# A trunk layer on one core: pools of their own for the first ffn_out's block sets, transposes at three norms at other steps, and groups of the mixing output that begin with the weight blocks still held

## The chip, the cores and the metric

The kernel runs on one core of one Trainium2 chip. The metric is the device time of one execution in microseconds (us). Three runs of the kernel before took 2295.66, 2296.3 and 2301.58 us; the median is 2296.3.

## The reference

One layer of an encoder trunk on 1024 tokens of width 1024, in float32: a half-step SwiGLU feed-forward part, a token mixing (retention in both directions, two-dimensional neighbourhood attention, gates), and a second feed-forward part, each between two RMS norms.

```python
def _rms_norm(x, gain):
    xf = x.astype(jnp.float32)
    y = xf * lax.rsqrt(jnp.mean(xf * xf, axis=-1, keepdims=True) + RMS_EPS)
    return (y * gain.astype(jnp.float32)).astype(x.dtype)

def _swiglu(x, w_in, w_out):
    g, u = jnp.split(x @ w_in, 2, axis=-1)
    return (jax.nn.silu(g) * u) @ w_out
...
    y_ret = (jax.nn.silu(rg) * y) @ w_ret_out
...
    merged = jax.nn.sigmoid(g_ret) * y_ret + jax.nn.sigmoid(g_na) * y_na
    return merged @ w_out
...
        h = _swiglu(_rms_norm(x, ffn1_pre_norm[l]), ffn1_w_in[l], ffn1_w_out[l])
        x = x + 0.5 * _rms_norm(h, ffn1_post_norm[l])
        m = _token_mixing(_rms_norm(x, mix_pre_norm[l]), w_mix_in[l], ret_decay_fwd[l], ret_decay_bwd[l],
                          na_rel_bias[l], w_ret_out[l], w_na_out[l], w_mix_out[l], pos)
        x = x + _rms_norm(m, mix_post_norm[l])
        h = _swiglu(_rms_norm(x, ffn2_pre_norm[l]), ffn2_w_in[l], ffn2_w_out[l])
        x = x + 0.5 * _rms_norm(h, ffn2_post_norm[l])
```

The hidden width of the feed-forward parts is 2816.

## The kernel before

**Precision.** Each float32 operand is split (`split`, L50) into a high part in fp32r, cast by ScalarE (L60), and a low part, the difference, by VectorE (L61). A product is three matmuls (`mm3`, L85, its lines L87 to L89): high by high, low by high, high by low. Names ending in h and l are such halves: wh and wl of a weight, gh and gl of a block of the hidden layer, a11h and a11l of an operand.

**Tokens.** The 1024 tokens are eight tiles of 128 rows, called tokens 0 to 7 here. Each stage begins with a norm and then *flips* a token: eight TensorE transposes (L126), four to a half, put the normalized rows into columns. `put` (L257) takes each half from its bank. For tokens 0 to 3 it is two splits. For tokens 4 to 7, ScalarE copies the first half (L272), and further sums (L276, L277, L282, L284, and L287, L288 on GpSimd) make the seven operands of a Strassen-Winograd scheme: a11, a12, a22, s1 to s4. Two banks, pt, serve the flips, six banks, ps, the products.

**ffn_in** (L404) computes the gate and up halves of the hidden layer in 22 steps, each with seven products of 12 matmuls. It stores blocks of the hidden layer (a11) and their sums to device memory, and beside that makes the four weight sums for ffn_out: `OutSums` (L509) loads four tiles tw, subtracts, and stores the result t. SyncE issues the loads (weights as wraw, blocks as graw), GpSimd the stores. Before the main loop, `lead` (L330) does the first two products of six of the steps, in between the norms of tokens 4 to 7; `norm_T` (L100) writes a normed token into tmp (L117).

**ffn_out** (L536) runs seven products over 11 blocks each. `Blocks` (L447) loads a block (graw) and splits it into gh and gl; which pool a set comes from goes round a list of four, and each pool reuses the memory of what was there before. In ffn_in 1's place lie, among others, the tiles tw; a set that lies over one must wait until the store that reads it has landed. While the last products run, the finished tokens go through stages (`Epilogue.steps`, L486): stage 0 sums the squares, 1 adds the residue (L494), 2 is the next norm (L505), 3 the flip. They lie in the list `later`, and one is taken per step. Tokens 4 to 7 finish last; their flips are done inside the mixing's first products by the loop at L1144, with 8 fillings of products in between. Before, all norms of 5, 6 and 7 stand at ffn_out's end.

**The mixing output** (`out_proj`, L136) goes through groups of tokens (0, 1, 2), (3, 4, 5), (6, 7). For each group it goes through the eight blocks k of the contraction; it loads and splits a weight block and the tokens' m (`stream`), and has the banks of the group's tokens summed. The last three k (`tail`) are kept, so that tokens end one after the other; each finished token goes through its epilogue (L219 to L230 on ScalarE, VectorE and, for tokens 6 and 7, GpSimd), its norm (L113, L117), and, `lag` products later, its flip.

The order on each engine is decided by a scheduler, from the order in which the code is written; `issue_after` holds an instruction behind a given one. Engines work through their queues in order.

## Time and profile before

| | |
|---|---|
| runs | 2295.66, 2296.3, 2301.58 us |
| the profiled execution | 2297.41 us |
| its span | 2295.6 us |
| mean granted clock | 0.991 |
| TensorE busy | 2216.4 us, 97% |
| VectorE, ScalarE, GpSimd busy | 1680.1, 1003.4, 591.6 us |

The span is what the profiler recorded from the first instruction to the last; 1.8 us of the execution lie around it. In the profile PE is TensorE, PEld its weight loads, DVE VectorE, ACT ScalarE, POOL GpSimd and SP SyncE; L with a number is a line of the kernel. A row of a window gives, for each engine, busy us and the count of its instructions, then the granted clock of TensorE (1.00 is full), the share of the DMA engines and GB/s. A row of waits gives who waits for whose result: us in total, times, the longest. A row of a timeline gives start, duration, the instruction, and in brackets the idle time before it and what ended that.

### The profile page before, as it was taken

To read this page: it belongs to the slowest core of one execution; us is meant where nothing else is said; L and a number is where in the kernel's file an instruction comes from. 1 tells how busy PE (TensorE), PEld (TensorE's weight loads), DVE (VectorE), ACT (ScalarE), POOL (GpSimd) and SP (SyncE) were. 2 spreads that over 40 slices of the span, in tenths; PEclk is the share of its full clock that TensorE was granted. 3 is DMA by queue.
4 is the path that set the end of the run, shared out by engine and by line. 5 is a ranking of instruction groups with operands and counts; after the bars stand their busy time and mean duration, and the time that the engine had idled before them with its cause. 6 is when DMAs were issued, how large, how long until landed. Compare 5 with 4: busy or idle time off the path is not lost.

```text
span 2295.6 us, 30372 instructions
## 1 busy us (share of the span) xinstructions
PE 2216.4 (97%) x10288; PEld 1838.0 (80%) x10288; DVE 1680.1 (73%) x2945; ACT 1003.4 (44%) x2102; POOL 591.6 (26%) x689
## 2 busy tenths in 40 slices
PE   6999999989998999999999999999799999999998
PEld 5788888768777887787888888887578888888886
DVE  7897777745778768969975688546899777776576
ACT  6333222334454322248885675315543222234453
POOL 5342424210124134411101222101533333331012
PEclk9999999999999999999999999999899999999999
DMA  5464545467664542257755476766545545447765
GB/s 183 148 215 142 174 144 176 153 217 235 196 208 137 179 166 103 92 182 244 223 176 172 150 228 233 277 230 206 180 157 177 181 145 183 134 167 232 235 199 184
DMA packets 163675, 422.63 MB, mean 184 GB/s; under 512 B 19712, under 2 KB 47488, under 8 KB 163456
## 3 DMA queue, kind: packets, MB, share of 16 engines
q1 hardware_dynamic: 130080, 310.04, 42.5%
q0 software_dynamic: 33440, 110.65, 12.5%
q8 instruction: 81, 1.33, 0.2%
q14 instruction: 74, 0.61, 0.1%
HBM read 301.60 MB, written 123.21 MB: 185 GB/s over the span
## 4 chain that ended last, share of the span: by engine, by line
PE 81%; DVE 11%; issue 3%; POOL 3%; ACT 1%; DMA 1%; POOLq 0%; DVEq 0%; SPq 0%; ACTq 0%
PE ps L89 25%; PE ps L87 25%; PE ps L88 25%; DVE wl L61 2%; PE pt L88 1%; PE pt L87 1%; PE pt L89 1%; PE ps L726 1%; POOL rstd L97 1%; PE pt L745 1%; POOL cmb L287 1%; POOL cmb L288 1%; DVE t L378 1%; DVE xs L494 1%; DVE tmp L117 1%
## 5 line engine op out<-in xcount | busy, mean ns | idle before, releaser
L61 DVE TENSOR_TENSOR wl<-wraw,wh 128x512 fp32r<-128x512 f32 x662 | 470.6, 730 | 77.8 <-ACT wh L60 76.9
L60 ACT CAST wh<-wraw 128x512 fp32r<-128x512 f32 x670 | 390.4, 618 | 218.5 <-PE ps L88 78.5
L87 PE MATMUL ps<-wh,gh 128*128 128x512 f32 x612 | 239.8, 393 | 13.2 <-ACT gh L60 12.0
L61 DVE TENSOR_TENSOR gl<-graw,gh 128x512 fp32r<-128x512 f32 (+2 forms) x178 | 128.4, 724 | 161.2 <-ACT gh L60 161.2
L88 PE MATMUL ps<-wl,gh 128*128 128x512 f32 x612 | 240.1, 393 | 2.0 <-DVE wl L61 2.0
L89 PE MATMUL ps<-wh,gl 128*128 128x512 f32 x612 | 239.4, 394 | 0.7 <-DVE gl L61 0.5
L60 ACT CAST gh<-graw 128x512 fp32r<-128x512 f32 (+2 forms) x178 | 106.6, 602 | 216.2 <-PE ps L88 86.8
L414 ACT ACTIVATE c<-c 128x512 f32<-128x512 f32 x88 | 55.7, 633 | 289.3 <-DVE c L384 206.4
L87 PEld LDWEIGHTS ps<-wh,gh 128*128 128x128 f32 x612 | 115.7, 189 | 39.1 <-ACT gh L60 13.1
L89 PEld LDWEIGHTS ps<-wh,gl 128*128 128x128 f32 x612 | 115.9, 190 | 28.0 <-DVE gl L61 3.9
L88 PEld LDWEIGHTS ps<-wl,gh 128*128 128x128 f32 x612 | 115.9, 190 | 25.9 <-DVE wl L61 2.7
L60 ACT CAST wh<-t 128x512 fp32r<-128x512 f32 x58 | 36.1, 622 | 201.8 <-DVE t L378 192.2
L484 POOL TENSOR_TENSOR q<-q,gain 128x512 f32<-128x512 f32 x22 | 33.6, 1544 | 348.7 <-ACT ps L483 334.4
L89 PE MATMUL ps<-a12h,wl 128*128 128x512 f32 x280 | 110.7, 395 | 3.7 <-DVE wl L61 3.7
L87 PE MATMUL ps<-a11h,wh 128*128 128x512 f32 x280 | 111.6, 399 | 1.4 <-ACT wh L60 0.7
L87 PE MATMUL ps<-a12h,wh 128*128 128x512 f32 x280 | 111.2, 397 | 0.0
L89 PE MATMUL ps<-a11h,wl 128*128 128x512 f32 x280 | 110.4, 394 | 0.7 <-DVE wl L61 0.7
L88 PE MATMUL ps<-a11l,wh 128*128 128x512 f32 x280 | 110.4, 394 | 0.0
L88 PE MATMUL ps<-a12l,wh 128*128 128x512 f32 x280 | 109.9, 392 | 0.0
L87 PE MATMUL ps<-a22h,wh 128*128 128x512 f32 x280 | 109.8, 392 | 0.0
L89 PE MATMUL ps<-a22h,wl 128*128 128x512 f32 x280 | 109.1, 390 | 0.0
L88 PE MATMUL ps<-a22l,wh 128*128 128x512 f32 x280 | 109.1, 389 | 0.0
(354 smaller groups left out, 5973.9 us busy)
## 6 DMA issues: line engine op xcount, KB each, us to landing
wraw<-in_dram SPq DMA_DIRECT2D x243, 512.0 KB, 4.4
tw<-in_dram SPq DMA_DIRECT2D x88, 256.0 KB, 3.3
t<-tw POOLq DMA_DIRECT2D x88, 256.0 KB, 4.1
wraw<-t SPq DMA_DIRECT2D x40, 512.0 KB, 3.8
g0s<-cmb POOLq DMA_DIRECT2D x44, 256.0 KB, 4.0
graw<-g0s SPq DMA_DIRECT2D x44, 256.0 KB, 2.9
g1s<-cmb POOLq DMA_DIRECT2D x44, 256.0 KB, 4.2
graw<-g1s SPq DMA_DIRECT2D x44, 256.0 KB, 2.8
```

Source lines behind the costliest of these rows:

```text
L60: nc.scalar.copy(h, src)
L61: (eng or nc.vector).tensor_tensor(l, src, hf, ALU.subtract)
L87: mm(ps, a[0], b[0], start=start, stop=False)
L88: mm(ps, a[0], b[1], start=False, stop=False)
L89: mm(ps, a[1], b[0], start=False, stop=stop)
L97: self.nc.gpsimd.tensor_tensor(r[:, :n], ms, self.mhalf[:, :n], ALU.pow)
L117: nc.vector.scalar_tensor_tensor(xn[:, bs], x[:, bs], r[:, 0:1], gain[:, bs], op0=ALU.mult, op1=ALU.mult)
L287: nc.gpsimd.tensor_tensor(s3, h2, s3, ALU.subtract)
L288: nc.gpsimd.tensor_tensor(s3, s3, l2, ALU.add)
L378: tt(t2, b22, t1, ALU.subtract)
L414: nc.scalar.activation(gate[j], gate[j], AF.Silu)
L484: (eng or c.nc.gpsimd).tensor_tensor(h if out is None else out, h, self.post[:, b * 512:(b + 1) * 512], ALU.mult)
```

## The change

Five things are changed.

1. **Block sets of the first ffn_out.** g0, g1 and g2 are the pools gl10, gl11 and gl12. The list of sets goes from (g0, g0, g0, g1) to (g0, g0, g1, g1), that of the raw blocks from (g2, g2, g1, g1) to (g2, g2, g0, g0), so that g1 holds sets alone. junk lies in front of them, two of the xs behind; tw is split into two pools of four tiles, for even and odd k.
2. **The start.** Tokens 0 to 3 are flipped at once, the flips of 4 to 7 are handed to `lead`, which does one after each of its pairs of products. tmp has four buffers instead of three; lead's results get a pool of their own.
3. **Stages in ffn_out.** A table, STAGES, mixes the stages of the four tokens instead of having token after token.
4. **Norms of tokens 6 and 7.** They are called in the flip loop, after the flips of tokens 4 and 5.
5. **The mixing output.** Each group but the first begins with the three weight blocks that the one before held, so 18 blocks are loaded instead of 24; the last group has a tail too; the flips are held behind the last matmul issued.

```diff
 RET_FILL = (14, 2, 2, 4, 2, 3, 0, 1, 2)
+STAGES = ((0, 0), (0, 1), (0, 2), (1, 0), (0, 3), (1, 1), (1, 2), (2, 0), (1, 3),
+          (2, 1), (2, 2), (3, 0), (3, 1), (2, 3), (3, 2), (3, 3))
 FLIP_FILL = (8, 8, 8, 8, 2)
 KEY_OFF = (0, 8, 24, 32)
...
         mm(ps, a[0], b[1], start=False, stop=False)
-        mm(ps, a[1], b[0], start=False, stop=stop)
+        return mm(ps, a[1], b[0], start=False, stop=stop)
         return self.psum.tile([P, 512], F32, tag=tag, name=tag, bufs=bufs)
...
-    def norm_T(self, x, gain, t, pool, put, ss=None):
+    def norm_T(self, x, gain, t, pool, put, ss=None, tmps=3):
...
         nc = self.nc
-        xn = pool.tile([P, D], F32, tag="tmp", name="tmp", bufs=3)
+        xn = pool.tile([P, D], F32, tag="tmp", name="tmp", bufs=tmps)
         if ss is None:
             for b in range(2):
...
-        left = []
-
-        def one(t, k, a, w):
+        left, last, mm = [], [], []
+
+        def one(t, k, a, w, start, stop):
             for e in [e for e in left if e[0] <= 0]:
                 left.remove(e)
-                f = e[1]()
+                with self.tc.issue_after(mm[0].ins):
+                    f = e[1]()
                 if f is not None:
             for b in range(2):
-                self.mm3(banks[t][b], a[t], w[b], k == 0, k == nk - 1)
+                mm[:] = [self.mm3(banks[t][b], a[t], w[b], start, stop)]
             for e in left:
...
             banks = {t: [self.bank() for _ in range(2)] for t in toks}
-            tl = tail if len(toks) > 1 else 0
-            for k in range(nk - tl):
-                w, a = wload(k), lhs(k, toks)
+            ks = [k for k, _, _ in last] + [k for k in range(nk) if k not in [e[0] for e in last]]
+            kept = {k: w for k, _, w in last}
+            for k in ks[:nk - tail]:
+                a = lhs(k, toks)
+                w = kept.pop(k) if k in kept else wload(k)
                 for t in toks:
-                    one(t, k, a, w)
-            last = [(k, lhs(k, toks), wload(k)) for k in range(nk - tl, nk)]
+                    one(t, k, a, w, k == ks[0], False)
+            last = [(k, lhs(k, toks), wload(k)) for k in ks[nk - tail:]]
             for t in toks:
                 for k, a, w in last:
-                    one(t, k, a, w)
+                    one(t, k, a, w, False, k == ks[-1])
                 f = done(t, banks[t])
                     left.append([max(lag, max([e[0] for e in left], default=-space) + space), f])
...
     def load(self, k):
-        self.b[k] = [self.tile() for _ in range(4)]
+        self.b[k] = [self.tile(k) for _ in range(4)]
         for t, src in zip(self.b[k], self.src):
...
     tt = nc.vector.tensor_tensor
-    later, rest, flips, xs = [], [], [], {}
+    later, rest, flips, xs, chains = [], [], [], {}, []
...
         ep.square(u, 0, q[3][:, u], b)
-        later.extend(stages(u, (q[3][:, u], q[2][:, u])))
+        chains.append(stages(u, (q[3][:, u], q[2][:, u])))
+        if u == 3:
+            later.extend(chains[t][j] for t, j in STAGES if j < len(chains[t]))
         g = ep.steps(t, xs[t], halves)
...
         if ep.pre is not None:
-            flips.extend(next(rest[j]) for j in ((), (), (0,), (1, 2, 3))[u])
+            flips.extend(next(rest[j]) for j in ((), (), (0,), (1,))[u])
                 ("a22", t_out[3], p4), ("a12", w_out[2], p2), ("s4", w_out[3], p3))
...
     assert not later
-    return flips
+    return flips, rest[2:]
 def stream(c, pool, src):
...
     apool = pool(right, "a1", "right")
-    early = pool(right, "early", "right")
+    early, leads = pool(right, "early", "right"), pool(right, "leads", "right")
     wx = Winograd(c, (apool,) * 3, early, (14,) * 7)
         nc.sync.dma_start(g, g1a)
+        flips = []
         for t in range(TT):
             nc.sync.dma_start(xt, x[t * P:(t + 1) * P, :])
-            f = c.norm_T(xt, g, t, ep, wx.put)()
-            if f is not None:
-                f()
+            flips.append(c.norm_T(xt, g, t, ep, wx.put, tmps=4))
+            if t < 4:
+                flips.pop()()
         fin = Pairs(c, wx, [(w1i[i], w1i[FT + i]) for i in LeftFactors.order], 3, 3)
-        fin.lead(lambda: early.tile([P, 512], F32, tag="lead", name="lead", bufs=6), on_pool=(3, 4, 5, 0))
+        fin.lead(lambda: leads.tile([P, 512], F32, tag="lead", name="lead", bufs=6), flips, (3, 4, 5, 0))
+        for f in flips:
+            f()
     with (tc.tile_pool(name="fin1", bufs=1, reuse_waits="tile") as fp,
-          tc.tile_pool(name="tw1", bufs=1, reuse_waits="tile") as tw):
+          tc.tile_pool(name="tw10", bufs=1, reuse_waits="tile") as tw0,
+          tc.tile_pool(name="tw11", bufs=1, reuse_waits="tile") as tw1):
         ffn_in(c, fin, fp, LeftFactors(c, early, gl[0]),
-               OutSums(c, lambda: tw.tile([P, 512], F32, tag="tw", name="tw", bufs=8), w1o, t1o))
+               OutSums(c, lambda k: (tw0, tw1)[k % 2].tile([P, 512], F32, tag="tw", name="tw", bufs=4), w1o, t1o))
     right.close()
     x0pool = pool(right, "x0", "right")
...
     q += [m0.tile([P, 4, 512], F32, tag="q", name="q", bufs=2) for _ in range(2)]
-    xs = [m0.tile([P, D], F32, name=f"xs{t}") for t in range(3)]
-    g1, g2, m1, g0 = (pool(mid, n) for n in ("gl11", "gl12", "mid1", "gl10"))
+    xs = [m0.tile([P, D], F32, name="xs0")]
+    m1, g1, g2, g0, m2 = (pool(mid, n) for n in ("mid1", "gl11", "gl12", "gl10", "mid2"))
     junk = [m1.tile([P, 512], F32, name=f"junk{u}") for u in range(4)]
-    xs.append(pool(mid, "mid2").tile([P, D], F32, name="xs3"))
-    rest = ffn_out(c, q, Blocks(c, (g0, g0, g0, g1), (g2, g2, g1, g1)), junk,
+    xs += [m2.tile([P, D], F32, name=f"xs{t}") for t in (1, 2)]
+    xs.append(pool(mid, "mid3").tile([P, D], F32, name="xs3"))
+    rest, norms = ffn_out(c, q, Blocks(c, (g0, g0, g1, g1), (g2, g2, g0, g0)), junk,
                    lambda t: xs[t] if t < 4 else ep.tile([P, D], F32, tag="xs", name="xs", bufs=4),
                    {n: (lambda j=j: ahead.update({j: c.load_w(wnv[j])})) for j, n in enumerate((65, 66))})
...
     evpool[:] = [wx.tmp, None]
-    for f, k in zip(rest, FLIP_FILL):
+    for n, k in enumerate(FLIP_FILL[:4]):
         fill(k)
-        f = f()
+        f = rest[n]()
+        if n < 2:
+            rest.append(next(norms[n]))
         if f is not None:
             f()
...
         ffn_in(c, fin, fp, LeftFactors(c, cmb, gl[1]),
-               OutSums(c, lambda: tw.tile([P, 512], F32, tag="tw", name="tw", bufs=8), w2o, t2o))
+               OutSums(c, lambda k: tw.tile([P, 512], F32, tag="tw", name="tw", bufs=8), w2o, t2o))
     left.close()
     g_stack.close()
```

What stands on ScalarE's queue at the end of ffn_in 1 and the start of ffn_out 1, where gh is the high half of a block (gh_3975 that of block 0, gh_4025 that of block 3), wh that of a weight, c a tile of the gate. Before:

```order
L60 CAST wh_4075<-wraw_4051 128x512
L60 CAST wh_4099<-wraw_4097 128x512
L414 ACTIVATE c1_3760<-c1_3760 128x512
L60 CAST wh_4121<-wraw_4097 128x512
L60 CAST gh_4025<-graw_4023 128x512
L60 CAST gh_3975<-graw_3973 128x512
L60 CAST gh_3987<-graw_3985 128x512
L60 CAST gh_3997<-graw_3995 128x512
```

Now the blocks 2 and 3 (gh_4008, gh_4036) are cast in the last but one step of ffn_in, blocks 0 and 1 far ahead of them in its early steps:

```order
L62 CAST wh_3774<-wraw_3768 128x512
L381 COPY c0_3617<-ps_3625 128x512
L62 CAST gh_4008<-graw_4006 128x512
L62 CAST gh_4036<-graw_4034 128x512
L419 ACTIVATE c0_3617<-c0_3617 128x512
```

The casts of the first four blocks have moved from behind the last weights' casts, where block 3's stood first, into ffn_in.

VectorE's queue at the flips of tokens 4 and 5 in the mixing start; q with xs is a norm of a token (xs_5531 and xs_5598 are tokens 6 and 7), cmb_6096 is a sum of token 4, cmb_6177 one of token 5. Before:

```order
L505 SCALAR_TENSOR_TENSOR q_3943<-xs_5531,rstd_6041,gain1_3934 128x512
L505 SCALAR_TENSOR_TENSOR q_3944<-xs_5531,rstd_6041,gain1_3934 128x512
L505 SCALAR_TENSOR_TENSOR q_3943<-xs_5598,rstd_6046,gain1_3934 128x512
L505 SCALAR_TENSOR_TENSOR q_3944<-xs_5598,rstd_6046,gain1_3934 128x512
L276 TENSOR_TENSOR cmb_6096<-a11h_5439,cmb_6095 128x512
L61 TENSOR_TENSOR a22l_6108<-pt_6101,a22h_6107 128x4x128
L277 TENSOR_TENSOR cmb_6096<-cmb_6096,a11l_5440 128x512
L282 TENSOR_TENSOR cmb_6106<-pt_6101,cmb_6095 128x512
L61 TENSOR_TENSOR wl_6227<-wraw_6220,wh_6226 128x512
L61 TENSOR_TENSOR s3l_6113<-cmb_6096,s3h_6112 128x4x128
L276 TENSOR_TENSOR cmb_6177<-a11h_5439,cmb_6176 128x512
L284 TENSOR_TENSOR cmb_6096<-pt_6101,cmb_6096 128x512
```

Now, with cmb_6098 the sum of token 4:

```order
L281 TENSOR_TENSOR cmb_6098<-a11h_5477,cmb_6097 128x512
L63 TENSOR_TENSOR a22l_6110<-pt_6103,a22h_6109 128x4x128
L282 TENSOR_TENSOR cmb_6098<-cmb_6098,a11l_5478 128x512
L287 TENSOR_TENSOR cmb_6108<-pt_6103,cmb_6097 128x512
L510 SCALAR_TENSOR_TENSOR q_3951<-xs_5542,rstd_6130,gain1_3942 128x512
L63 TENSOR_TENSOR s3l_6115<-cmb_6098,s3h_6114 128x4x128
L510 SCALAR_TENSOR_TENSOR q_3952<-xs_5542,rstd_6130,gain1_3942 128x512
L289 TENSOR_TENSOR cmb_6098<-pt_6103,cmb_6098 128x512
```

The norm of token 6 stands between the sums of token 4 and no longer in front of them, that of token 7 comes after these rows; the lines L276 to L288 of before are L281 to L293 now.

TensorE's queue at the flip of token 5 in the mixing output (tmp_15858 before, tmp_15840 now), with the products of tokens 6 and 7 around it. Before:

```order
L88 MATMUL ps_15867<-wl_15945,gh_15949 128x512
L89 MATMUL ps_15867<-wh_15944,gl_15950 128x512
L87 MATMUL ps_15864<-wh_15995,gh_16004 128x512
L87 MATMUL ps_15865<-wh_15999,gh_16004 128x512
L87 MATMUL ps_15866<-wh_15995,gh_16004 128x512
L87 MATMUL ps_15867<-wh_15999,gh_16004 128x512
L126 MATMUL pt_16039<-ident_69,tmp_15858 128x128 x4
L126 MATMUL pt_16049<-ident_69,tmp_15858 128x128 x4
L88 MATMUL ps_15864<-wl_15996,gh_16004 128x512
```

Now:

```order
L91 MATMUL ps_15848<-wh_15953,gl_15947 128x512
L89 MATMUL ps_15849<-wh_15957,gh_15946 128x512
L90 MATMUL ps_15849<-wl_15958,gh_15946 128x512
L91 MATMUL ps_15849<-wh_15957,gl_15947 128x512
L128 MATMUL pt_15991<-ident_69,tmp_15840 128x128 x4
L89 MATMUL ps_15846<-wh_15983,gh_15976 128x512
L90 MATMUL ps_15846<-wl_15984,gh_15976 128x512
L89 MATMUL ps_15847<-wh_15987,gh_15976 128x512
L89 MATMUL ps_15848<-wh_15983,gh_15976 128x512
L128 MATMUL pt_16001<-ident_69,tmp_15840 128x128 x4
```

The flip has moved behind eight more matmuls of the group (wl_15954 and others of the kept or early blocks), and its halves have four matmuls between them.

## The prediction

> **What bounds the kernel now.** I read the profile's page first, then the share of each engine by windows, then what TensorE waits for, then the timeline at each of its longer waits. The page's rows for TensorE and for the chain that ended last:
>
> ```profile
> PE 2216.4 (97%) x10288; PEld 1838.0 (80%) x10288; DVE 1680.1 (73%) x2945; ACT 1003.4 (44%) x2102; POOL 591.6 (26%) x689
> ...
> PE 81%; DVE 11%; issue 3%; POOL 3%; ACT 1%; DMA 1%; POOLq 0%; DVEq 0%; SPq 0%; ACTq 0%
> ```
>
> TensorE is busy for 2216.4 of 2295.6 us: 79.2 us are its idle time, and the change takes away no matmul. So a gain can come only from that idle time and from what follows it at a lower clock. Where it lies is in the windows; the first window below is one of full pace:
>
> ```profile
> 200.00:300.00 100.00, 100.00 (x443) 82.81 (x442) 71.78 (x116) 30.02 (x53) 29.41 (x38) 1.00 0.48 164
> 400.00:500.00 100.00, 88.80 (x384) 72.94 (x383) 58.38 (x93) 33.73 (x60) 23.68 (x30) 0.95 0.54 182
> ...
> 700.00:750.00 50.00, 42.99 (x184) 34.43 (x183) 44.78 (x60) 21.60 (x39) 24.05 (x22) 0.93 0.42 134
> ...
> 1600.00:1650.00 50.00, 40.72 (x166) 30.40 (x165) 41.78 (x64) 27.85 (x66) 24.39 (x21) 0.86 0.52 166
> 1650.00:1700.00 50.00, 43.61 (x194) 34.24 (x193) 44.77 (x64) 24.26 (x49) 20.09 (x16) 1.00 0.46 152
> ```
>
> The first number in brackets counts matmuls: 443 in 100 us is 0.2257 us each. In the other windows TensorE lost time, and in the last three VectorE is busy for 84 to 90%. What TensorE waited for, in total, times and longest, has these at its head:
>
> ```profile
> PE pt L126 <- DVE tmp L117: 19.7, 6, 8.6
> PE ps L87 <- ACT gh L60: 12.0, 2, 11.2
> ```
>
> The first are transposes that wait for a norm, the second is one wait of 11.2 us where the first ffn_out begins. The change works at both kinds of place.
>
> **Start of ffn_out 1.** The timeline at that wait:
>
> ```profile
> 458.57 10.57 SPq L458 DMA_DIRECT2D graw<-g0a  x4
> ...
> 461.65 0.56 POOL L67 DMA_DIRECT2D t<-tw  x1
> ...
> 466.85 2.18 ACT L60 CAST gh<-graw 128x512 fp32r<-128x512 f32 x4 [9.53 <-DMA graw<-g0a]
> ...
> 468.04 0.79 PE L87 MATMUL ps<-wh,gh 128*128 128x512 f32 x1 [11.20 <-ACT gh L60]
> ```
>
> ScalarE's first cast in its queue is the one of gh_4025, whose raw block lies over buffers of tw that a late store still reads; gh_3975, which TensorE needs first, stands behind it although it needs no such store. After the change the casts of the first four blocks stand in ffn_in, in memory that is free by then (tw is in two pools, and only the half that ends earlier lies under a set), and the eight weight pieces fit their buffers, so nothing that the first matmul reads is behind that store. What it costs now: the window 400:500 holds 384 matmuls instead of 443, 59 x 0.2257 = 13.3 us (11.2 of waiting, the rest at a low clock). I take the whole 13.3 as gained. Bounds: 11 to 14. What could take its place: the four casts and four subtractions (0.62 and 0.68 us each) go into a stage where the window 200:300 shows VectorE at 72% and TensorE at 100%, so they hide. One of them, gl_4009, has to wait for the landing of a store of tw, and an eviction stands behind it on VectorE. The page's median from issue to landing is
>
> ```profile
> t<-tw POOLq DMA_DIRECT2D x88, 256.0 KB, 4.1
> ```
>
> A product is 12 matmuls, 2.7 us, and there are six banks, so TensorE reaches that bank later than the wait can last: 0, at worst 4.1 - 2.7 = 1.4 us. SyncE's queue gets four more waits for a store (a rival, below).
>
> **Start of the kernel.** Four tokens are flipped at once, the flips of the others go between the lead products. Three waits lie where the order changes:
>
> ```profile
> 39.86 0.66 PE L126 MATMUL pt<-ident,tmp 128*128 128x128 f32 x4 [1.11 <-DVE tmp L117]
> ...
> 44.30 0.63 PE L126 MATMUL pt<-ident,tmp 128*128 128x128 f32 x4 [2.18 <-DVE tmp L117]
> ...
> 61.79 0.50 PE L89 MATMUL ps<-a12h,wl 128*128 128x512 f32 x1 [1.40 <-DVE wl L61]
> ```
>
> They sum to 4.7 us. A product of 12 matmuls now lies between two flips, which covers the norms. But the second half of token 6's flip now waits for ScalarE's copy of its first half, queued behind the cast of s4h of an earlier token, which waits for two combinations on GpSimd: by the nearest rows (mixing output, below) 2 x 1.66 and a cast of 0.62, less five matmuls (1.1 us) that TensorE has in between, a wait of 2.8 us. So 4.7 - 2.8 = 1.9, taken as 2 us gained. Bounds: 6.7 gained (4.7, and a low clock after them) to 3 lost.
>
> **Transposes inside ffn_out 1.** Flips of tokens 0 and 2 wait:
>
> ```profile
> 629.26 1.42 DVE L505 SCALAR_TENSOR_TENSOR q<-xs,rstd,gain 128x512 f32<-128x512 f32 x2 [0.45 <-POOL rstd L97]
> 630.16 1.07 PE L126 MATMUL ps<-ident,q 128*128 128x128 f32 x6 [2.25 <-DVE q L505]
> ...
> 657.84 1.27 PE L126 MATMUL pt<-ident,q 128*128 128x128 f32 x8 [1.90 <-ACT pt L483]
> ```
>
> The new list of stages puts the flip of token 0 one step later (12 matmuls, 2.7 us, over 2.25) and that of token 2 two steps later (5.4 over 1.90). Both waits go: 4.15. Token 3's flip keeps its step and now follows token 2's after two steps; for its banks I take off 0.5. So 3.65 gained, between 2 and 4.15.
>
> **Mixing start.** VectorE and TensorE around the flip of token 5, and the flip of token 6:
>
> ```profile
> 699.84 1.41 DVE L505 SCALAR_TENSOR_TENSOR q<-xs,rstd,gain 128x512 f32<-128x512 f32 x2 [0.44 <-POOL rstd L97]
> ...
> 701.14 0.60 PE L126 MATMUL pt<-ident,q 128*128 128x128 f32 x4
> 701.68 1.41 DVE L505 SCALAR_TENSOR_TENSOR q<-xs,rstd,gain 128x512 f32<-128x512 f32 x2 [0.43 <-POOL rstd L97]
> 703.01 0.68 DVE L276 TENSOR_TENSOR cmb<-a11h,cmb 128x512 f32<-128x512 f32 x1
> ...
> 706.08 0.66 PE L126 MATMUL pt<-ident,q 128*128 128x128 f32 x4 [3.41 <-ACT cmb L272]
> ...
> 707.22 0.68 DVE L284 TENSOR_TENSOR cmb<-pt,cmb 128x512 f32<-128x512 f32 x1
> ...
> 724.45 1.01 PE L126 MATMUL pt<-ident,q 128*128 128x128 f32 x4 [2.00 <-DVE cmb L284]
> ```
>
> The four L505 are the norms of tokens 6 and 7; now they stand after the combinations of token 4 have begun, so L276 takes the place of the first of them without its wait of 0.44: about 699.4 instead of 703.01. Eight instructions (two of them L505), at about 0.64 us each, lead from there to the end of token 4's last read of its bank, at about 704.5. Token 5's second half now waits for that read and comes with four matmuls (0.9 us) fewer done before it: 706.08 - 704.5 - 0.9 = 0.7 gained; a wait of about 2.9 stays. For token 6 the same count on VectorE, with two instructions slowed by GpSimd, ends at 722.0, and TensorE comes at 721.6: a wait of 0.4 instead of 2.00. What a wait costs after it is seen in the clock (the last but two of the columns):
>
> ```profile
> 468.00:472.00 4.00, 3.96 (x9) 3.02 (x10) 1.99 (x4) 1.02 (x2) 0.00 (x0) 0.51 0.91 306
> ...
> 707.50:710.90 3.40, 3.40 (x9) 2.67 (x8) 3.40 (x7) 1.74 (x3) 1.05 (x1) 0.50 0.57 212
> ...
> 724.50:727.90 3.40, 3.40 (x11) 2.82 (x12) 3.40 (x6) 1.53 (x3) 2.10 (x2) 0.51 0.68 145
> ```
>
> After the waits of 3.41 and 2.00 the granted clock was half for 3.4 us, 1.7 us lost each time. The first of them stays, the second goes with its wait. Sum: 0.7 + 1.6 + 1.7 = 4.0 gained, between 1 and 7.
>
> The Trainium skill ("TensorE: Matmul & The Clock Gate", part 1) says that the clock halves after at least one idle window of about 3.4 us. By that rule the waits of 2.9 here and of 2.1 below would leave it whole, and the forecast would be 3.4 us lower, 2263; the row after a wait of 2.00 differs from it, and I go by the row.
>
> **Mixing output.** Six loads of weights are left out, with 12 casts and 12 subtractions, by the page's means:
>
> ```profile
> L61 DVE TENSOR_TENSOR wl<-wraw,wh 128x512 fp32r<-128x512 f32 x662 | 470.6, 730 | 77.8 <-ACT wh L60 76.9
> L60 ACT CAST wh<-wraw 128x512 fp32r<-128x512 f32 x670 | 390.4, 618 | 218.5 <-PE ps L88 78.5
> ```
>
> That is 8.8 us of VectorE and 7.4 of ScalarE, in a stretch where VectorE is the late engine. It isn't the gain: a subtraction is worth something only where TensorE waits behind it. The waits there, and the stretch after the longest:
>
> ```profile
> 1624.07 1.09 PE L126 MATMUL pt<-ident,tmp 128*128 128x128 f32 x4 [4.20 <-DVE tmp L117]
> ...
> 1625.70 0.68 DVE L61 TENSOR_TENSOR wl<-wraw,wh 128x512 fp32r<-128x512 f32 x1
> ...
> 1625.86 1.66 POOL L276 TENSOR_TENSOR cmb<-a11h,cmb 128x512 f32<-128x512 f32 x1 [2.73 <-ACT cmb L272]
> ...
> 1627.99 1.75 DVE L61 TENSOR_TENSOR wl<-wraw,wh 128x512 fp32r<-128x512 f32 x1
> ```
> ```profile
> 1622.00:1636.00 14.00, 8.72 (x22) 5.53 (x23) 13.54 (x16) 3.75 (x7) 8.83 (x6) 0.51 0.37 124
> ```
> ```profile
> PE pt L126 <- DVE tmp L117: 7.8, 3, 4.2
> ```
>
> Token 5's flip comes eight matmuls later (1.8 us), while its norm, which ends a chain of VectorE, ScalarE and GpSimd, ends only about 0.6 us sooner, since the stored combinations of token 4 still stand in front of it. The wait shrinks from 4.20 to about 2.1: 2.1 gained. Behind it TensorE ran 8.72 us of work at half clock; with a wait of 2.1 I expect 3.4 us of that, so (8.72 - 3.4) / 2 = 2.7 gained, which four subtractions fewer (0.68 to 1.75 us each) allow VectorE to feed. The other two waits for a norm sum to 7.8 - 4.2 = 3.6; the kept weights are ready, so TensorE comes to token 6's flip later beside its chain: I take 2.0 of the 3.6. Sum 6.8 gained; bounds 0 (VectorE no less late) and 12.
>
> **The sum** is 13.3 + 2 + 3.65 + 4.0 + 6.8 = 29.75 us. Against the profiled execution, 2297.41 us (span 2295.6 and 1.8 around it), it gives 2267.7; the median of the runs shown, 2296.3, is 1.1 lower, so I forecast 2266.6, rounded 2267.
>
> **The rivals.**
> The mixing output gives nothing: more transposes' work of VectorE meets GpSimd in fewer us, and each subtraction there takes 1.75 instead of 0.68 as in the rows above. Against it speaks that VectorE has fewer instructions in all. Time: 2267 + 6.8 = 2274, with a start that loses 3 as well 2279. (The Trainium skill, "GPSIMD Engine Reference", section 8, has GpSimd share its SBUF interfaces with VectorE where that reads two SBUF inputs; the two rows agree.)
> Half or all of the 11.2 us stays: something else is late at ffn_out's first matmul, a weight piece or a block of the fourth load. For it speaks that four loads of blocks still stand at the end of ffn_in; against it that the first six are issued long before. Time: 2274 to 2280.
> The slower end: SyncE's queue. The four new loads of blocks in ffn_in each wait for the landing of a store issued in the same step, in front of the next steps' weight loads. If each holds them back so long that TensorE stops for the store's 4.1 us and runs 3.4 us at half clock, that is 4 x 5.8 = 23.2, and with blocks as late as before the 13.3 isn't won: 2266.6 + 36.5 = 2303. It decides once a wait outlasts the time that a landed load lies unread. Against it: the L60 row has the casts wait mostly for TensorE to free their buffers, not for loads, and two such loads stand in ffn_in before the change, where TensorE idled 0.15 us in all:
>
> ```profile
> 74.00:456.00 382.00, 381.85 (x1686) 315.85 (x1685) 295.15 (x465) 119.30 (x208) 124.82 (x153) 1.00 0.50 169
> ```
>
> That the change doesn't do what it says is ruled out for the order, which shows the casts and flips at their new places; that all terms but one come out near nothing stays as a small chance.
>
> **How the numbers follow.** Forecast 0.70, mixing output without gain 0.13, the start of ffn_out partly late 0.10, all near nothing 0.04, the slower end 0.03. The unknown terms go to both sides by 2 to 7 us each and are independent: about 8 below and 9 above; to the rivals at 2279 and 2280 the range reaches up: 2258 to 2281. A measurement of this kernel tells about 0.3%, 6.9 us, from no change: faster 0.93, the same 0.04, slower 0.03.
>
> **What would show it.** Right: no wait for gh over 1 us near 457 and 443 matmuls in the 100 us there; no waits at the flips of tokens 0 and 2; token 6's flip in the mixing start under 1 us; token 5's in the mixing output about 2; VectorE some 9 us less busy. Wrong: a wait for wl, gh or a landing of more than 3 us at ffn_out's start; new waits between 74 and 456; the half clock in the mixing output as long as before; waits at the start that sum to more than the 4.7.

## The result and the profile after

The changed kernel takes 2280.97 us (median of 4 runs, 2278.87 to 2282.71), the kernel before 2297.26 us beside it (4 runs, 2295.66 to 2301.58): a ratio of 0.9926, 95% interval 0.9909 to 0.9943, 16.3 us faster. The profiled execution took 2280.88 us with a span of 2279.1. A second set of runs, for the experiments, gave 2278.27 us (4 runs) beside 2298.23 (9 runs), ratio 0.9915 (0.9901 to 0.9928). The forecast was 2267, with a range of 2258 to 2281: the sign is as predicted, the gain is a little over half of the 29.75 us of the sum. The time lies 0.03 us inside the slow end of the range. That end was put there for two rivals, and the stages below show neither of them; that the time still falls inside is luck.

From the page of the changed kernel, then its windows (busy time of TensorE, its weight loads, VectorE, ScalarE and GpSimd, then the granted clock), then what TensorE waits for:

```profile
PE 2212.2 (97%) x10288; PEld 1837.1 (81%) x10288; DVE 1681.9 (74%) x2933; ACT 996.2 (44%) x2090; POOL 591.6 (26%) x689
```
```profile
400.00:500.00 100.00, 100.00 (x443) 82.81 (x442) 67.04 (x99) 38.65 (x68) 23.23 (x28) 1.00 0.59 198
700.00:750.00 50.00, 42.77 (x180) 34.30 (x179) 36.37 (x51) 16.05 (x29) 17.79 (x18) 0.93 0.45 151
```
```profile
PE ps L90 <- DVE wl L63: 5.9, 3, 4.4
...
PE ps L89 <- ACT ev L381: 5.6, 1, 5.6
...
PE ps L733 <- ACT qh L65: 3.9, 1, 3.9
```

The wait for gh is gone and 400:500 holds 443 matmuls, the full pace. But the window 700:750, in the mixing start, holds 180 matmuls where it held 184 (of other work, as the changed kernel is 12 to 18 us ahead there), and two waits stand in the list that weren't there in this length: 5.6 us for a copy `ev` (L381) and 4.4 us for a subtraction `wl`.

To see where time came and went I took instructions that both executions have and compared their starts. One group of rows is from the timeline of before:

```profile
101.89 0.68 DVE L384 TENSOR_TENSOR c<-ps,c 128x512 f32<-128x512 f32 x1
...
694.45 0.20 DVE L489 TENSOR_SCALAR ss<-ss 128x1 f32<-128x1 f32 x1
...
742.83 0.69 DVE L381 TENSOR_TENSOR ev<-ps,ev 128x512 f32<-128x512 f32 x1 [0.81 <-PE ps L89]
...
1479.08 1.37 DVE L1292 TENSOR_TENSOR m<-ps,m 128x512 f32<-128x512 f32 x2 [1.44 <-PE ps L89]
...
1684.14 0.68 DVE L381 TENSOR_TENSOR gt<-ps,c 128x512 f32<-128x512 f32 x1
```

The same instructions in the timeline of the changed kernel:

```profile
99.32 0.68 DVE L389 TENSOR_TENSOR c<-ps,c 128x512 f32<-128x512 f32 x1
...
676.24 0.20 DVE L494 TENSOR_SCALAR ss<-ss 128x1 f32<-128x1 f32 x1
...
728.32 0.69 DVE L386 TENSOR_TENSOR ev<-ps,ev 128x512 f32<-128x512 f32 x1 [3.51 <-PE ps L91]
...
1467.06 1.37 DVE L1306 TENSOR_TENSOR m<-ps,m 128x512 f32<-128x512 f32 x2 [1.19 <-PE ps L91]
...
1667.57 0.68 DVE L386 TENSOR_TENSOR gt<-ps,c 128x512 f32<-128x512 f32 x1
```

The first row lies behind the start, the second where token 7's norm of ffn_out 1's result begins (the moved norms, L505 and now L510, come after it), the third where the first mixing job's first sum leaves its bank, the fourth ahead of the mixing output, the fifth in the second ffn_in. The lead of the changed kernel is 2.57, 18.21, 14.51, 12.02 and 16.57 us at them. Of the 18.21 at the second, 13.3 are the 59 matmuls that 400:500 won. So, against the forecast:

| stage | forecast | measured |
|---|---|---|
| start | 2 | 2.57 |
| start of ffn_out 1 | 13.3 | 13.3 |
| flips inside ffn_out 1 | 3.65 | 2.3 (18.21 - 2.57 - 13.3) |
| mixing start | 4.0 | -3.7 (14.51 - 18.21) |
| between, untouched | 0 | -2.5 (12.02 - 14.51) |
| mixing output | 6.8 | 4.55 (16.57 - 12.02) |

The longest wait in the untouched stages is 3.9 us for qh (2.65 before), and in three other runs below the same wait is 3.12, 4.43 and 2.00. The changed kernel run again below takes 736.93 us from the third row to the fourth, against 738.74 here and 736.25 before: most of the 2.5 us is the spread from one execution to the next, and no run shows that the change has a part in it.

The mixing start lost time although the two flips wait less, as the timeline of TensorE shows, and then the timeline of all engines at its end:

```profile
686.26 0.63 PE L128 MATMUL pt<-ident,q 128*128 128x128 f32 x4 [2.72 <-DVE cmb L289]
704.29 0.63 PE L128 MATMUL pt<-ident,q 128*128 128x128 f32 x4 [0.81 <-DVE cmb L289]
```
```profile
716.10 0.68 DVE L63 TENSOR_TENSOR s2l<-cmb,s2h 128x512 fp32r<-128x512 f32 x1
...
716.86 3.45 POOL L292 TENSOR_TENSOR cmb<-a12h,cmb 128x512 f32<-128x512 f32 x1 [5.43 <-DVE s2l L63]
717.31 1.28 DVE L63 TENSOR_TENSOR wl<-wraw,wh 128x512 fp32r<-128x512 f32 x2
718.51 0.68 DVE L400 TENSOR_TENSOR wraw<-wraw,t 128x512 f32<-128x512 f32 x1
720.39 1.26 POOL L293 TENSOR_TENSOR cmb<-cmb,a12l 128x512 f32<-128x512 f32 x1
721.69 0.62 ACT L62 CAST s4h<-cmb 128x512 fp32r<-128x512 f32 x1 [4.33 <-POOL cmb L293]
722.21 0.58 ACT L381 COPY ev<-ps 128x512 f32<-128x512 f32 x1
...
722.84 0.80 PE L89 MATMUL ps<-s2h,wh 128*128 128x512 f32 x1 [5.64 <-ACT ev L381]
```

Read from below: TensorE's next product needs a bank, which the copy `ev` empties. The copy's bank had been ready, but in ScalarE's queue it stands behind the cast s4h of token 7, and s4h waits for two sums on GpSimd (L292, L293). The first sum follows token 7's s2l on VectorE, and takes 3.45 us beside VectorE's `wl` and L400, which run at 0.64 to 0.68 us each. In the kernel before the same chain ran when TensorE came later, and the wait was 0.82 us:

```profile
739.76 0.50 PE L87 MATMUL ps<-s2h,wh 128*128 128x512 f32 x1 [0.82 <-ACT ev L376]
```

The low clock that follows, in windows of the changed kernel:

```profile
687.10:690.50 3.40, 3.40 (x10) 2.64 (x9) 3.40 (x6) 0.65 (x2) 2.87 (x3) 0.51 0.19 77
721.30:728.10 6.80, 5.26 (x12) 3.81 (x12) 1.47 (x2) 2.14 (x4) 1.63 (x2) 0.50 0.44 132
```

TensorE's 5.26 us of work at half clock are 2.6 us lost on top of the 5.64. The flips won 3.41 + 2.00 - 2.72 - 0.81 = 1.9, and the low clock after the second of them, 1.7 (the clock is at 1.00 from 704.3 to 707.7 now); the copy took 5.64 - 0.82 = 4.8 and 2.6. That is 3.8 lost, and the rows above say 3.7.

### The profile page after: what moved, and what is told of

It is laid out like the page before. It is cut to its first block, busy times and chain, and to the rows that moved or that the text cites. A ratio compares the mean times of both kernels' runs of the same rounds, so it can differ in the third digit from the quotient of the medians.

```text
span 2279.1 us, 30322 instructions
## 1 busy us (share of the span) xinstructions
PE 2212.2 (97%) x10288; PEld 1837.1 (81%) x10288; DVE 1681.9 (74%) x2933; ACT 996.2 (44%) x2090; POOL 591.6 (26%) x689
## 3 DMA queue, kind: packets, MB, share of 16 engines
q0 software_dynamic: 33440, 110.65, 12.5%
## 4 chain that ended last, share of the span: by engine, by line
PE 78%; DVE 11%; issue 4%; POOL 3%; ACT 2%; DMA 1%; SPq 0%; DVEq 0%; POOLq 0%; ACTq 0%
PE ps L91 24%; PE ps L89 24%; PE ps L90 24%; DVE wl L63 2%; PE pt L91 1%; PE pt L90 1%; PE pt L89 1%; PE ps L733 1%; POOL cmb L292 1%; PE pt L752 1%; POOL cmb L293 1%; POOL rstd L99 1%; DVE xs L499 1%; DVE t L383 1%; DMA wraw<-in_dram 0%
## 5 line engine op out<-in xcount | busy, mean ns | idle before, releaser
L62 ACT CAST wh<-wraw 128x512 fp32r<-128x512 f32 x658 | 383.8, 617 | 223.9 <-PE ps L90 79.5
L63 DVE TENSOR_TENSOR gl<-graw,gh 128x512 fp32r<-128x512 f32 (+2 forms) x178 | 134.7, 758 | 142.9 <-ACT gh L62 140.1
```

The source lines that it names most:

```text
L62: nc.scalar.copy(h, src)
L63: (eng or nc.vector).tensor_tensor(l, src, hf, ALU.subtract)
```

## Experiments

My theory after the two traces: VectorE bounds the mixing start. From token 7's norm (the second row above) to its s2l it took 734.44 - 694.45 = 40.0 us before and 716.10 - 676.24 = 39.9 us after, so waits of TensorE inside it are moved and not removed; and the chain through s4h blocks ScalarE's queue behind it. Two rivals: the norms at their new place cost by themselves; or the chain through s4h is what costs and VectorE's count of instructions is not. The measure for this stage is the stretch from token 7's norm to the first `ev` row: 48.38 us before (742.83 - 694.45), 52.08 after (728.32 - 676.24).

**The sets alone.** Before, with the pools of the changed kernel (the sets, tw, the banks put by):

```diff
-    g1, g2, m1, g0 = (pool(mid, n) for n in ("gl11", "gl12", "mid1", "gl10"))
+    m1, g1, g2, g0, m2 = (pool(mid, n) for n in ("mid1", "gl11", "gl12", "gl10", "mid2"))
...
-    rest = ffn_out(c, q, Blocks(c, (g0, g0, g0, g1), (g2, g2, g1, g1)), junk,
+    rest = ffn_out(c, q, Blocks(c, (g0, g0, g1, g1), (g2, g2, g0, g0)), junk,
```

> The kernel before with the pools alone: the sets of ffn_out 1 over pools of their own, the tw buffers in two pools, the six banks that are put by in a pool of their own; the order of norms, stages and the mixing output as before. My theory: the whole of the first term and nothing else, since the stages behind keep their order and each only starts earlier: 2297.3 - 13.3 = 2284.0 us, 443 matmuls in the window 400:500, and the waits of 2.25, 1.90, 2.00, 3.41 and 4.20 us all still there. Rival (part of the 13.3 is given back in the mixing start, because VectorE there is late whatever TensorE does): 2286 to 2290.

Measured: 2284.76 us (5 runs), ratio 0.9943 (0.9929 to 0.9956), 12.5 us less than the 2297.23 beside it. The window 400:500 holds 443 matmuls here too: the first term is right and stands alone. A little is given back: the wait of 0.82 for the copy `ev` is 2.39 us here, and the mixing start's stretch is 49.9 us instead of 48.4. The flip of token 6 waits 2.33 us here and the clock stays full behind it (1.00 from 712.7 to 716.1), so TensorE comes earlier to the copy and waits there instead.

**The norms where they stood.** The changed kernel with tokens 6 and 7 normed at the end of ffn_out 1:

```diff
-            flips.extend(next(rest[j]) for j in ((), (), (0,), (1,))[u])
+            flips.extend(next(rest[j]) for j in ((), (), (0,), (1, 2, 3))[u])
...
-    return flips, rest[2:]
+    return flips, []
...
-        if n < 2:
-            rest.append(next(norms[n]))
```

> The changed kernel with the norms of tokens 6 and 7 back at the end of ffn_out 1, as they stood before. Theory (the mixing start is bound by VectorE's work from its end of ffn_out 1 to token 7's last sum, 40.0 us before and 39.9 after, and moving two norms within it neither adds nor removes work): 2279 to 2283 us, no difference that can be told from 2281.0, and the 5.64 us wait for the first copy out of a bank still there in some form. Rival (the norms at their new place are what made the 5.64 us wait): about 2281.0 - 7.7 = 2273 (3.7 lost instead of 4.0 gained). My forecast had it the other way: 2285, 4.0 slower.

Measured: 2275.47 us (4 runs, 2273.91 to 2277.93), ratio 0.9906 (0.9893 to 0.9920). By its median it is faster than either set of runs of the changed kernel, but the intervals overlap (0.9901 to 0.9928 for the second), so the trace has to decide. The end of its mixing start in the timeline:

```profile
718.20 1.67 POOL L292 TENSOR_TENSOR cmb<-a12h,cmb 128x512 f32<-128x512 f32 x1 [3.64 <-DVE s2l L63]
718.65 3.44 DVE L63 TENSOR_TENSOR wl<-wraw,wh 128x512 fp32r<-128x512 f32 x2
719.95 1.59 POOL L293 TENSOR_TENSOR cmb<-cmb,a12l 128x512 f32<-128x512 f32 x1
721.57 0.62 ACT L62 CAST s4h<-cmb 128x512 fp32r<-128x512 f32 x1 [2.87 <-POOL cmb L293]
722.10 0.58 ACT L381 COPY ev<-ps 128x512 f32<-128x512 f32 x1
...
722.73 0.50 PE L89 MATMUL ps<-s2h,wh 128*128 128x512 f32 x1 [2.39 <-ACT ev L381]
```

In the trace the moved norms lose, then, with the sign of the rival and against my theory of no difference. What VectorE needs is the same (717.44 - 677.39 = 40.05 us to s2l), but L292 takes 1.67 us here and not 3.45, and it is VectorE's two subtractions beside it that are slow (3.44 us for two, 1.28 in the changed kernel). Counted from token 7's norm, TensorE comes 2.0 us later to the copy (42.95 against 40.96), having waited 3.41 and 2.06 at the flips. The stretch is 49.99 us (727.38 - 677.39), 2.1 shorter. The other runs below that keep the norms at their new place, and the chain and VectorE's work there as they are, take 50.98 to 52.12, so 1.0 to 2.1 us lie in this stage. The rest of the difference of the medians (2.8 or 5.5, by the set of runs) lies in stages that the edit doesn't touch.

**The mixing output of before.** The changed kernel without kept blocks:

```diff
-            ks = [k for k, _, _ in last] + [k for k in range(nk) if k not in [e[0] for e in last]]
-            kept = {k: w for k, _, w in last}
-            for k in ks[:nk - tail]:
-                a = lhs(k, toks)
-                w = kept.pop(k) if k in kept else wload(k)
+            tl = tail if len(toks) > 1 else 0
+            for k in range(nk - tl):
+                w, a = wload(k), lhs(k, toks)
```

> The changed kernel with the mixing output of before: no kept weight blocks, groups from block 0, no tail in the last group, no order edge at the transposes. Theory: the trace shows 4.2 to 4.5 us gained in that stage, so 2281.0 + 4.3 = 2285.3, with the wait of 4.20 us for token 5's norm back and the 4.40 us wait for a subtraction gone. The forecast's term: 2287.8. Rival (the gain there is owed to the earlier start of the stage, not to the kept blocks): 2281.

Measured: 2283.02 us (5 runs, 2282.24 to 2283.54), ratio 0.9938 (0.9925 to 0.9950), 2.1 or 4.8 us slower than the changed kernel by its two sets of runs. The time from the fourth row of the first table of rows to the fifth is 204.54 us (1464.96 to 1669.50), against 200.51 in the changed kernel and 205.06 before. So the edit is worth 4.0 us in that stage, the wait of 4.20 is back as 4.27, and the one of 4.40 is gone. Without the order edge at the transposes every engine's queue reads row for row as with it, so that edge is no cause and wasn't run apart.

**The stages token after token.**

```diff
-        chains.append(stages(u, (q[3][:, u], q[2][:, u])))
-        if u == 3:
-            later.extend(chains[t][j] for t, j in STAGES if j < len(chains[t]))
+        later.extend(stages(u, (q[3][:, u], q[2][:, u])))
```

> The changed kernel with the epilogue's stages token after token, as before, in place of the list. Theory by the landmarks of the two traces: 2.3 us lost inside ffn_out 1, so 2283.3, with the waits of about 2.25 and 1.90 us at the flips of tokens 0 and 2 back and those of 0.93 and 0.95 gone. The forecast's term: 2284.6. Rival (what is lost there is won back in the mixing start, which VectorE bounds): 2281.

Measured: 2281.26 us (5 runs), ratio 0.9930 (0.9917 to 0.9942): by the time alone it can't be told from the changed kernel. In the trace the waits of 2.25 and 1.86 are back, and token 7's norm comes at 679.03, 2.0 to 2.8 us later than in the two executions of the changed kernel, of which its own start is 0.0 to 0.5 late. The mixing start has the same 5.64 us wait and nearly the same stretch (51.8), so the 2 us are kept up to there; the medians (0.3 and 3.0 us above those of the changed kernel) are too far spread to show them.

**The cast s4h on GpSimd**, so that ScalarE's queue waits for GpSimd no longer:

```diff
-        return lambda: c.split(*self.part("s4", ts), s3, eng=nc.gpsimd)
+        def s4():
+            h, l = self.part("s4", ts)
+            nc.gpsimd.tensor_copy(h, s3)
+            nc.gpsimd.tensor_tensor(l, s3, h.bitcast(F32), ALU.subtract)
+        return s4
```

Beside it the changed kernel ran again.

> The changed kernel itself, to stand beside the next three on one chip: 2281 us (2279 to 2283), and the wait of 5.64 us at the first copy out of a bank in the mixing start again.

Measured: 2278.27 us (4 runs, 2276.88 to 2279.63), and the wait is 5.63.

> The changed kernel with the rounding cast of s4 (the last sum of a token's flip) on GpSimd, which makes that sum, in place of ScalarE, so that ScalarE's queue no longer waits for GpSimd. Theory (the waits that the change removed came back at instructions that stand behind this cast in ScalarE's queue: the first copy out of a bank in the mixing start, s1h and with it a subtraction in the mixing output, the copies of a21 at the start): the 5.64 us wait falls under 1.5 with the low clock after it, the 4.40 us one under 2.5, those of 1.26 and 2.53 at the start under 1; together 8 to 14 us, so 2267 to 2273. Rival (these waits are VectorE's own lateness and ScalarE's queue only shows it): the waits appear at another line with about the same length, 2278 to 2282. Second rival (two more GpSimd instructions' worth of work per token delays its sums): 2283 or more.

Measured: 2283.84 us (5 runs), ratio 0.9939 (0.9926 to 0.9951), slower by 5.6 than the changed kernel beside it. The place in question:

```profile
718.95 3.45 POOL L292 TENSOR_TENSOR cmb<-a12h,cmb 128x512 f32<-128x512 f32 x1 [4.23 <-DVE s2l L63]
722.48 1.26 POOL L293 TENSOR_TENSOR cmb<-cmb,a12l 128x512 f32<-128x512 f32 x1
723.80 0.61 POOL L296 CAST s4h<-cmb 128x512 fp32r<-128x512 f32 x1
724.49 1.26 POOL L297 TENSOR_TENSOR s4l<-cmb,s4h 128x512 fp32r<-128x512 f32 x1
725.79 0.58 ACT L385 COPY ev<-ps 128x512 f32<-128x512 f32 x1 [6.34 <-POOL s4l L297]
...
726.43 0.80 PE L89 MATMUL ps<-s2h,wh 128*128 128x512 f32 x1 [6.92 <-ACT ev L385]
```

This run doesn't test the queue. With the cast moved, the ring of four `cmb` buffers turned differently, and the copy's buffer came to lie over the sum that s4l still reads (6.34 us for s4l L297). In the changed kernel it lies over token 7's s1, which is free. A change of engine moved a buffer, and the copy waits for the end of the same chain by another way. The second rival, more work on GpSimd, isn't excluded either: it is its time that came, and only 0.9 of the 5.6 us lie in this stretch (53.04 us against 52.11), 1.3 in the mixing output (201.63 against 200.29) and 0.7 at the start. What the run does show: in the mixing output the wait of 4.4 us for `wl` is 4.42 with no s4h in ScalarE's queue. My theory for that wait, s1h standing behind s4h, is wrong.

> The same cast on GpSimd, and the norms of tokens 6 and 7 back at the end of ffn_out 1. If moving the norms is worth something once nothing stands behind the cast, this is slower than the run with the cast alone by 2 to 4 us (the waits of 3.41 and 2.06 at the flips of tokens 5 and 6 in place of 2.72 and 0.81, and one low-clock stretch); if the stretch is bound by VectorE all the same, equal within 1.5 us; if the moved norms cost by themselves, 2 us or more faster.

Measured: 2278.72 us (4 runs), ratio 0.9919 (0.9906 to 0.9933). Here the buffer of the copy lies as in the changed kernel, and no wait for the first copy is left:

```profile
720.03 1.67 POOL L292 TENSOR_TENSOR cmb<-a12h,cmb 128x512 f32<-128x512 f32 x1 [3.63 <-DVE s2l L63]
720.43 0.58 ACT L385 COPY ev<-ps 128x512 f32<-128x512 f32 x1
```

The copy runs beside L292; with the cast on ScalarE and the norms at the same place it came after both sums, and TensorE waited 2.39 us for it. So it is the place behind s4h in ScalarE's queue that holds the copy. But the first sum out of a bank is late instead (2.58 us for `ev` L390) and the flip of token 6 waits 2.58. The stretch is 49.3 us, 0.7 less than the 49.99 with the cast on ScalarE, and another 0.7 is lost at the start of the kernel, where a flip waits 3.16 us for a sum. Beside the run before it, with the norms moved, it is 5.1 us faster, 3.7 of it in this stretch; buffers and norms both differ there, and the two aren't told apart.

**VectorE's work itself.** For tokens 4 to 7 of the mixing start the subtraction of s1 is done three times:

```diff
         c.split(*self.part("s1", ts), s1)
+        if self.spill is not None:
+            h, l = self.part("s1", ts)
+            for _ in range(2):
+                nc.vector.tensor_tensor(l, s1, h.bitcast(F32), ALU.subtract)
```

> The changed kernel with the subtraction of s1 done three times instead of once for tokens 4 to 7 of the mixing start: eight more VectorE instructions of about 0.6 us, the same values again. Theory (VectorE bounds the stretch from the last norms to token 7's last sum): the whole 4.9 us (and more where a two-input subtraction meets GpSimd) comes through to the end, 2285 to 2289. Rival (the stretch is bound by a chain with slack on VectorE): under 1.5 us, 2281 to 2282.5.

Measured: 2280.00 us (5 runs), ratio 0.9922 (0.9906 to 0.9936), 1.7 more than the changed kernel beside it. The eight instructions, as a group (ns of the shortest, the middle and the longest, first and last start), and both ends of the stretch:

```profile
L294 DVE TENSOR_TENSOR s1l<-cmb,s1h x8: 675/678/686, 687.8 to 717.4; 128x512 fp32r<-128x512 f32 x8
```
```profile
676.70 0.21 DVE L498 TENSOR_SCALAR ss<-ss 128x1 f32<-128x1 f32 x1
...
728.83 0.69 DVE L390 TENSOR_TENSOR ev<-ps,ev 128x512 f32<-128x512 f32 x1 [0.24 <-PE ps L91]
```

8 x 0.678 = 5.4 us of VectorE more, and the stretch is 52.13 us against 52.11 in the changed kernel beside it (729.11 - 677.00): 0.0. The 1.7 of the medians isn't in that stage. TensorE waits at other places (1.93 at a flip; 1.20, 0.94, 2.17 and 1.07 for `wl`), the copy no more: the added work filled the 5.63 us in which TensorE would have waited for the copy. So the theory that VectorE's count of instructions alone bounds this stretch falls, though VectorE is then the engine that TensorE waits for. s2l of token 7 came only 1.4 us later, since sums of the first mixing job that had stood ahead of it now stand behind it.

**The chain shortened.** Token 7's last two sums, L292 and L293, on VectorE:

```diff
-        nc.gpsimd.tensor_tensor(s3, h2, s3, ALU.subtract)
-        nc.gpsimd.tensor_tensor(s3, s3, l2, ALU.add)
+        eng = nc.vector if self.spill is not None and t == 7 else nc.gpsimd
+        eng.tensor_tensor(s3, h2, s3, ALU.subtract)
+        eng.tensor_tensor(s3, s3, l2, ALU.add)
```

> The changed kernel with the last two sums of token 7's flip in the mixing start (the operand of s4's cast) on VectorE in place of GpSimd; nothing else changes places in ScalarE's queue, and the buffers are the same. Theory (the 5.64 us wait is the chain s2l on VectorE, two sums on GpSimd of which the first is slowed to 3.45 us by VectorE's neighbours, the cast s4h, and behind it in ScalarE's queue the copy that TensorE needs): the copy starts about 2.4 us earlier, the wait falls from 5.6 to about 3.2 and the low clock after it from 6.8 to 3.4 us, 2.4 + 1.7 = 4.1 us, so about 2275.5 (2274 to 2278) where the changed kernel gave 2281.0 and 2278.3. Rival (VectorE's own lateness): two more VectorE instructions make the next weight pieces later and the wait returns at another line, 2279 to 2282.

Measured: 2274.29 us (4 runs, 2273.70 to 2276.01), ratio 0.9900 (0.9883 to 0.9916). The timeline, and the window behind the wait:

```profile
717.36 0.68 DVE L293 TENSOR_TENSOR cmb<-a12h,cmb 128x512 f32<-128x512 f32 x1
...
718.57 0.68 DVE L294 TENSOR_TENSOR cmb<-cmb,a12l 128x512 f32<-128x512 f32 x1
...
719.28 0.62 ACT L62 CAST s4h<-cmb 128x512 fp32r<-128x512 f32 x1 [1.87 <-DVE cmb L294]
719.80 0.58 ACT L382 COPY ev<-ps 128x512 f32<-128x512 f32 x1
...
720.44 0.80 PE L89 MATMUL ps<-s2h,wh 128*128 128x512 f32 x1 [3.21 <-ACT ev L382]
```
```profile
720.40:723.80 3.40, 3.36 (x8) 2.69 (x9) 1.59 (x3) 1.14 (x2) 1.19 (x1) 0.50 0.31 61
```

The wait is 3.21 us and the low clock 3.4 long, both as expected, and the stretch is 48.76 us (725.06 - 676.30), 3.3 shorter. Counted from token 7's norm, the copy starts 2.5 us earlier and the wait is 2.4 us shorter. With the copy freed by the cast on GpSimd above, that settles the cause of the 5.64 us: the chain s2l, two sums, s4h, copy. The other 0.9 us is less certain, since the low clock changes by itself: in the run with the mixing output of before, 3.4 us of it went with the same 5.64.

> The same two sums on VectorE, and the norms of tokens 6 and 7 back at the end of ffn_out 1. By the runs before, the old place of the norms has waits of 3.41, 2.06 and 2.39 in the mixing start against 2.72, 0.81 and 5.64. If what made the moved norms lose was the 5.64 alone, this is no faster than the run with the sums on VectorE and the norms moved: 2273 to 2276, of which the 2.39 gives about 1. If the old place is better by itself, it is 3 us faster than that run.

Measured: 2274.34 us (4 runs, 2272.04 to 2277.76), ratio 0.9902 (0.9887 to 0.9917). The two are equal by their medians, but the stretch is 47.39 us here, still 1.4 shorter than with the norms moved. So the chain behind the moved norms is part of what they lose; how much they cost by themselves, the two executions don't tell, since stretches of the same work differ by 1.1 us above. Both kernels are faster than the one before (1.0%), and by their medians 4 to 7 us faster than the changed one.

**The mixing output: stretched instructions, or their number.** First, the sums of s3 of tokens 4 and 5 on VectorE in place of GpSimd:

```diff
-    wx.s3_on_pool = (4, 5)
```

> The changed kernel with the sums of s3 for tokens 4 and 5 of the mixing output on VectorE in place of GpSimd (four instructions, 0.68 us each when alone, about 1.6 each on GpSimd). Theory (VectorE is the late engine there because its instructions with two operands in SBUF take 1.5 to 1.78 us beside GpSimd's and 0.68 alone): 4 x 0.68 = 2.7 us more work, some four to six stretched instructions fewer at 0.8 to 1.1 us each, so 0.5 to 4 us faster, and the wait of 4.40 us for a subtraction shorter. Rival (VectorE's count of instructions decides, not their stretching): 2 to 3 us slower, and the 4.40 us wait longer.

Measured: 2277.55 us (4 runs), ratio 0.9917 (0.9902 to 0.9932). The 4.40 us wait is 3.07, one of 1.76 is 3.96 instead; the stage takes 200.03 us, 0.3 to 0.5 less. The sign is that of the theory, the size is too small to tell from nothing. Then the 12 subtractions that the kept blocks leave out, put back alone:

```diff
+                held = k in kept
-                w = kept.pop(k) if k in kept else wload(k)
+                w = kept.pop(k) if held else wload(k)
+                for h, l in w if held else ():
+                    j = self.wpool.tile([P, 512], F32, tag="t2", name="t2", bufs=1)
+                    self.nc.vector.tensor_tensor(j, h.bitcast(F32), l.bitcast(F32), ALU.subtract)
```

> The changed kernel with the VectorE work of the 12 left-out subtractions put back in the mixing output, without the loads and casts: wherever a weight piece is still held, one subtraction of its two halves into a scratch tile that nobody reads. The run with the mixing output of before lost 4.0 to 4.3 us in that stage against the changed kernel. Theory (VectorE's count of instructions is what the stage is short of): all of it is lost again with the subtractions alone, 3.5 to 6 us in that stage, 2282 to 2286 in all. Rival (the loads and ScalarE's casts were what cost, or the gain is only the order of the groups): under 1.5 us in that stage, 2278 to 2282.

Measured: 2278.87 us (5 runs), ratio 0.9920 (0.9907 to 0.9934). The 12 as a group, and the long wait, which is as in the changed kernel:

```profile
L166 DVE TENSOR_TENSOR t<-wh,wl x12: 680/688/692, 1532.9 to 1582.7; 128x512 f32<-128x512 f32 x12
```
```profile
1619.31 0.50 PE L90 MATMUL ps<-wl,gh 128*128 128x512 f32 x1 [4.39 <-DVE wl L63]
```

The stage takes 200.33 us (1465.32 to 1665.65), against 200.29 in the changed kernel run for the experiments (1466.04 to 1666.33): 12 x 0.688 = 8.3 us of VectorE cost nothing. They stand between 1533 and 1583, ahead of the long waits, which lie behind 1600. The subtractions of the run with the mixing output of before stand there too, for the most part: it has 31 subtractions of weights between 1520 and 1600, the changed kernel 22. So the 4.0 us are not VectorE's time for the 12 subtractions. Whether they come from the loads, from ScalarE's casts or from the order in which the groups begin, no run here tells.

## Why the prediction was right and where it wasn't

**Start of ffn_out 1** (13.3): right in size and reason. No wait for gh is left near 457, 443 matmuls fill the 100 us, and alone the sets give 12.5 in the median. Neither a load's queue nor a subtraction took its place, and the slower end, SyncE's queue, did not come.

**Start of the kernel** (2): 2.57, in part by luck. The three old waits are gone, and the new wait at token 6's flip is 2.53 where the text has 2.8. But a second one, 1.26 at token 5's flip, was not in the sum:

```profile
41.10 0.66 PE L128 MATMUL pt<-ident,tmp 128*128 128x128 f32 x4 [1.26 <-ACT cmb L277]
49.54 0.66 PE L128 MATMUL pt<-ident,tmp 128*128 128x128 f32 x4 [2.53 <-ACT cmb L277]
```

What makes up for it is a low clock of 3.4 us that stood before (0.50 from 45.3 to 48.7, 1.6 us lost) and doesn't come in this execution. It does come in the changed kernel run again, where the lead at the first row is 2.15 us.

**Flips inside ffn_out 1** (3.65): the mechanism is right, 2.25 and 1.90 are gone. The 0.5 that I took off for banks was too little: two later flips wait 0.93 (for ScalarE's squares, which go into that bank) and 0.95 (for a subtraction that reads it), and the term is 2.3.

**Mixing start** (+4.0): wrong in sign, -3.7. The step that failed is the count "for token 6 ... a wait of 0.4 instead of 2.00", taken as a gain. The flips did come to 2.72 and 0.81, near the 2.7 that the text's own sum gives (3.41 - 0.7; it says 2.9) and its 0.4. But the sum ended at token 6. I did not ask what is late next when TensorE gets through the flips earlier: the copy of the first mixing job, whose place in ScalarE's queue is behind s4h of token 7. The row of 0.82 us for `ev` stood in the trace of before, as the sign of a chain that ended just in time; each us that TensorE gains ahead of it is a us of waiting there. The moved norms then made it worse, since L292 met VectorE at another moment and took 3.45 us.

**Mixing output** (6.8): 4.55, and the run without the edit says 4.0. Its 2.1 at token 5's flip was too small (the 4.20 us wait went altogether), and the other two waits for a norm went from 3.6 to 1.91 us, near the 2.0; but the low clock did not go with it: it follows the 4.40 us wait for a subtraction that takes its place. The sentence "which four subtractions fewer ... allow VectorE to feed" failed: most of the subtractions that were left out had stood where VectorE had time. Nor is VectorE 9 us less busy: it is busy for 1681.9 us against 1680.1, with 12 instructions fewer, and the subtractions `wl` that are left take 741 ns in the mean instead of 730.

**Between**: 2.5 us that no term held, most of them the spread between executions.

The Trainium skill ("TensorE: Matmul & The Clock Gate", part 1) has the clock halve after at least one idle window of about 3.4 us. The trace of after doesn't agree either: the window behind the wait of 2.72 us is at 0.51. By that rule the forecast would have been 2263, further off.

## What to carry to other kernels

When a wait is removed, follow the engine that was waiting to the next place where it needs another engine, and look there for a wait of a few tenths: it shows a chain that ended just in time and that now takes the gain. Look at what stands ahead in the queue of the engine that frees the buffer, and not only at the buffer. And work that is left out is worth something only at its own place: look up in the trace when it ran, before it is priced by the stretch beside it.
